# A hybrid decoder layer on one Trainium2 core: the first half's first two output-projection blocks made together, and a reordered piece of the first stage

## The chip, the cores and the metric

The kernel runs on one core of a Trainium2 chip. The metric is the device time of one execution in microseconds; the kernel before has a median of 2079.53 us over 3 runs (2077.59 to 2079.88). The profiled execution took 2081.88 us, of which 2080.0 us lie between its first and its last instruction. The engines are named as in the profile: PE (TensorE) multiplies matrices, PEld is its weight load, DVE is VectorE, ACT is ScalarE, POOL is GpSimd, SP issues the transfers, DMA carries them out.

## The reference, cut to what matters

One layer, 1024 tokens, width 1024, float32. Three branches share one input projection, are merged by sigmoid gates, and go through one output projection; a convolutional feed-forward block follows.

```
h = rms_norm(x, norm_mix_pre)
z = h @ w_in
y_pool = pool_branch(z_pool) @ w_proj_pool
y_mem  = mem_attention(z_q, mem_n) @ w_proj_mem
dw, da, dg = low-rank parts of the token-shifted z     # 64, 64 and 128 columns
w_log = -softplus(-(w0 + tanh(dw) @ w_up_decay)) - 0.5  # decay
a     = sigmoid(a0 + da @ w_up_a)
g     = sigmoid(dg) @ w_up_g                            # gate
y_rwkv = rwkv_branch(r, k, v, decay, a, g) @ w_proj_rwkv
gates  = sigmoid(z_gate + gate_b)
merged = gates[0] * y_pool + gates[1] * y_rwkv + gates[2] * y_mem
x = x + rms_norm(merged @ w_o, norm_mix_post)
u = causal_dwconv(rms_norm(x, norm_ffn_pre) @ w_ffn_up)
x = x + rms_norm((gelu(u_gate) * u_val) @ w_ffn_down, norm_ffn_post)
```

Two lines matter here: `tanh(dw)` and `sigmoid(dg)`, which are made in the first stage, and `merged @ w_o`.

## The kernel before, in words

Everything is held transposed: channels on the 128 partitions, tokens along the row. The 1024 channels are 8 rows of 128 (k = 0 to 7), the tokens two halves of 512 (n = 0, 1). A product of float32 quality is made of three PE passes with operands that are split into a high part and a rest: `mm3` (L165 to L171) does high by high (L168), rest of the activation by high weight (L169) and high activation by rest of the weight (L170). One output block (128 channels by 512 tokens) with all 8 rows is thus 24 matmuls into one PSUM bank; `gemm` (L173) runs over the rows.

Weights: `load_w` brings a block of 8 rows in four transfers of two rows each, issued by SP into `wraw` (3 buffers), then splits each: ACT makes the high part `whi` (L129), POOL the rest `wlo` (L132), 4 buffers each. There are two classes of all these buffers and of the PSUM banks (`g0`, `g1`, two banks each); successive blocks take the classes in turn. So the weights of one block can be prepared while another block is multiplied.

The stages around the change:

- First stage, `start()` (L367): the low-rank columns go into `lu` (decay part in partitions 0 to 63, the other in 64 to 127) and `gr` (gate). ACT makes tanh on the decay part; high parts and rests of it go into `la` and `ld` (L391, L392), the operands of two small products that come later, in `rwkv_group` (L454, L455). ACT also makes the sigmoid of `gr`, and its two parts go into `gl`, the operand of the gate's product `gl` by `w_up_g` right after it.
- `merge(n, js)` (L938): for output block j of half n, the product `y_rwkv` by `w_proj_rwkv` (8 rows, 24 matmuls), times the sigmoid of a gate `g` (L948), plus the other two branches' part (L949), then split by ACT into `mgh` (L122) and by DVE into `mgl` (L123). Block j of the merge is row k = j of the next product.
- `wo_gemm(n, js)` (L1106): the output projection, 8 blocks, each over the 8 rows `mgh`, `mgl`. Each finished block is copied to `o` by DVE (L1117), and its square is made by ACT (L1088 for block 0, L1091 for the others) and summed by DVE (L1092).
- After that the second half's merge begins, and the first half's residual and norm run beside it.

The program calls `merge(0, range(8))`, `wo_gemm(0, range(8))`, `merge(1, range(1))` and so on in this order. Within it, a scheduler sets the order of instructions on each engine from the code's order and from its own estimate of when operands are ready; each engine then works strictly through its row. The helper `two_gemms` (L289) makes two blocks together: rows 0 to `late`-1 of the first, the same rows of the second, then the remaining rows of the first and of the second. It is used in `merge(0, ...)`, for the first two blocks, with `late` = 6, and in `wo_gemm(1, ...)`, for the first two blocks, with `late` = 7.

## Time and profile before

| what | value |
|---|---|
| median of 3 runs | 2079.53 us (2077.59 to 2079.88) |
| the profiled execution | 2081.88 us, span 2080.0 us |
| PE busy | 2014.5 us, 97% of the span, 12246 matmuls |
| PEld | 1558.7 us, 75% |
| DVE, ACT, POOL busy | 1361.4 us (65%), 1069.4 us (51%), 812.5 us (39%) |
| mean granted TensorE clock | 0.992 of full speed |
| first half's output projection | first matmul at 1232.88 us, the next stage's first at 1281.30 us |
| last merge block's split of the first half | ACT at 1239.62 us, DVE at 1240.27 us |

In a timeline row, the first number is the start in us from the span's start, the second the duration; then the engine, the line, what is written and read, and in brackets the idle time before it and what ended it. Consecutive matmuls overlap in these rows: each is shown 0.39 us long, while the next starts 0.23 us after it. The distance between two starts is the time that one costs. In a list of waits the three numbers are the sum in us, the count and the longest.

### The profile page before, as it was taken

How to read it: one execution, taken by the hardware profiler on the slowest of the kernel's cores; microseconds unless marked ns; L12 is line 12 of the kernel's file. 1: busy time of each engine (PE TensorE's matmuls, PEld its weight loads, DVE VectorE, ACT ScalarE, POOL GpSimd, SP SyncE). 2: the span in 40 equal slices, each digit the busy share in tenths (PEclk: the TensorE clock that was granted, in tenths of full speed). 3: DMA queues.
4: the chain of work that ended last, by engine and by line, in shares of the span. 5: the costliest groups of instructions: out<-in, count | busy, mean ns of one | idle time of the engine just before them, and what ended most of it. 6: DMA issues, size and time to landing. Idle time of an engine off the chain costs nothing.

```text
span 2080.0 us, 34125 instructions
## 1 busy us (share of the span) xinstructions
PE 2014.5 (97%) x12246; PEld 1558.7 (75%) x12246; DVE 1361.4 (65%) x2170; ACT 1069.4 (51%) x2249; POOL 812.5 (39%) x917
## 2 busy tenths in 40 slices
PE   8999999999999999999999999998999999989997
PEld 5777767776778667866878878876678777767886
DVE  6567437664667357823895443778777777767798
ACT  7585348623773367434566243546444443444644
POOL 5521213121222121212133355655588888832341
PEclk9999999999999999999999999999999999999999
DMA  4312211120212021214427343634322222169776
GB/s 155 130 41 74 67 59 61 65 82 22 87 61 98 24 89 61 78 51 133 160 82 234 123 142 110 213 123 135 109 72 76 79 74 83 64 189 261 166 181 149
DMA packets 176713, 221.83 MB, mean 107 GB/s; under 512 B 16544, under 2 KB 128288, under 8 KB 176544
## 3 DMA queue, kind: packets, MB, share of 16 engines
q1 hardware_dynamic: 163616, 204.44, 30.3%
q0 software_dynamic: 11856, 14.16, 4.2%
q8 instruction: 97, 1.59, 0.3%
q10 hardware_dynamic: 1072, 1.05, 0.2%
q14 instruction: 72, 0.59, 0.1%
HBM read 170.30 MB, written 49.28 MB: 106 GB/s over the span
## 4 chain that ended last, share of the span: by engine, by line
PE 30%; DVE 7%; DMA 5%; POOL 4%; issue 4%; ACT 3%; SPq 0%; POOLq 0%; ACTq 0%; DVEq 0%
PE psg L170 5%; PE psg L169 5%; PE psg L168 5%; POOL wt L1028 2%; PE psd L169 2%; PE psd L170 2%; PE psf L170 2%; PE psd L168 2%; PE psf L169 2%; PE psf L168 2%; POOL sm L1013 1%; DMA a<-in_w_fup 1%; DMA g<-d_zg 1%; DMA R<-d_f 1%; POOL wlo L132 1%
## 5 line engine op out<-in xcount | busy, mean ns | idle before, releaser
L132 POOL TENSOR_TENSOR wlo<-wraw,whi 128x256 fp32r<-128x256 f32 x472 | 411.6, 881 | 941.8 <-ACT whi L129 775.1
L168 PE MATMUL psg<-hh,whi 128*128 128x512 f32 x928 | 380.7, 410 | 2.7 <-DVE kv L315 2.7
L170 PE MATMUL psg<-hh,wlo 128*128 128x512 f32 x928 | 376.9, 406 | 0.2
L169 PE MATMUL psg<-hl,whi 128*128 128x512 f32 x928 | 375.8, 405 | 0.0
L129 ACT CAST whi<-wraw 128x256 fp32r<-128x256 f32 x472 | 182.7, 403 | 220.8 <-PE psg L169 108.0
L168 PEld LDWEIGHTS psg<-hh,whi 128*128 128x128 f32 x928 | 174.7, 188 | 43.3 <-DVE kv L315 4.0
L170 PEld LDWEIGHTS psg<-hh,wlo 128*128 128x128 f32 x928 | 174.5, 188 | 43.2 <-POOL wlo L132 5.3
L169 PEld LDWEIGHTS psg<-hl,whi 128*128 128x128 f32 x928 | 174.7, 188 | 39.5 <-issue 3.4
L1028 POOL TENSOR_TENSOR wt<-a,wt 128x256 fp32r<-128x256 f32 x136 | 133.8, 1013 | 31.3 <-ACT wt L1027 31.3
L168 PE MATMUL psd<-f,u 128*128 128x512 f32 x292 | 115.8, 397 | 8.2 <-ACT f L1355 4.8
L169 PE MATMUL psd<-f,u 128*128 128x512 f32 x292 | 115.6, 396 | 0.6 <-DVE f L1359 0.6
L170 PE MATMUL psd<-f,u 128*128 128x512 f32 x292 | 115.2, 396 | 0.0
L1028 POOL TENSOR_TENSOR wt<-sm,wt 128x256 fp32r<-128x256 f32 x102 | 106.8, 1066 | 19.2 <-ACT wt L1027 19.2
L170 PE MATMUL psf<-h2h,wt 128*128 128x512 f32 x272 | 108.8, 400 | 1.0 <-POOL wt L1028 0.6
L168 PE MATMUL psf<-h2h,wt 128*128 128x512 f32 x272 | 106.3, 391 | 1.7 <-ACT wt L1027 1.6
L169 PE MATMUL psf<-h2l,wt 128*128 128x512 f32 x272 | 106.0, 390 | 0.0
L1027 ACT CAST wt<-sm 128x256 fp32r<-128x256 f32 x102 | 37.9, 404 | 129.4 <-POOL sm L1013 124.1
L1046 DVE SCALAR_TENSOR_TENSOR d<-z,pv,d 128x1023 f32<-128x1023 f32 x68 | 91.6, 1347 | 12.0 <-ACT d L1044 9.5
L170 PE MATMUL psf<-t,wt 128*128 128x512 f32 x204 | 80.8, 396 | 3.4 <-POOL wt L1028 3.4
L686 DVE TENSOR_TENSOR HV<-ph,Hd 64x128 f32<-64x128 f32 x112 | 32.4, 289 | 72.2 <-PE ph L640 48.0
L168 PE MATMUL psf<-t,wt 128*128 128x512 f32 x204 | 79.6, 390 | 0.0
L169 PE MATMUL psf<-t,wt 128*128 128x512 f32 x204 | 79.5, 390 | 0.0
(424 smaller groups left out, 4750.7 us busy)
## 6 DMA issues: line engine op xcount, KB each, us to landing
wraw<-in_w_in SPq DMA_DIRECT2D x240, 128.0 KB, 2.4
a<-in_w_fup SPq DMA_DIRECT2D x128, 128.0 KB, 2.4
d_zg<-st SPq DMA_DIRECT2D x48, 256.0 KB, 2.7
wraw<-in_w_fup SPq DMA_DIRECT2D x80, 128.0 KB, 2.5
fw<-in_w_fdn SPq DMA_DIRECT2D x33, 256.0 KB, 4.2
fraw<-d_f SPq DMA_DIRECT2D x33, 256.0 KB, 5.3
wraw<-in_w_prwkv SPq DMA_DIRECT2D x64, 128.0 KB, 2.4
wraw<-in_w_o SPq DMA_DIRECT2D x64, 128.0 KB, 2.5
```

The costliest lines, as they stand in the source:

```text
L129: last_whi[0] = A.copy(hi, src).ins
L132: (V if lo_on_dve[0] else G).tensor_tensor(lo, src, hi.bitcast(F32), op=ALU.subtract)
L168: first = PE.matmul(ps, wh, xh, start=start, stop=False)
L169: PE.matmul(ps, wh, xl, start=False, stop=False)
L170: last_mm[0] = PE.matmul(ps, wl, xh, start=False, stop=stop).ins
L686: ready = V.tensor_tensor(HV[q, :, c + 1, e], ph[q], Hd[q], op=ALU.add).ins
L1013: eng.tensor_tensor(out_[u], a[u], b[u], op=op)
L1027: A.copy(w[0][:, us], src[u])
L1028: last_low[0] = G.tensor_tensor(w[1][:, us], src[u], w[0][:, us].bitcast(F32), op=ALU.subtract).ins
L1046: V.scalar_tensor_tensor(d[:, n:], z[:, :T - n], col(cw, j), d[:, n:], op0=ALU.mult, op1=ALU.add)
```

## The change

Two edits. In `wo_gemm` the condition `n == 1 and j == 0` becomes `j == 0`: the first half's first two blocks are now made by `two_gemms` as well, with rows 0 to 6 of both ahead of row 7 of both. In `start()`, the five lines that make the tanh and the operands `la` and `ld` stand behind the gate's product instead of ahead of the gate's sigmoid.

```diff
@@ start() @@
             scaled(ev, 512, gemm(load_w(w_in[16 + 8 * c], KC, c=c), hrhs(512)))
-        act(u[0:64], u[0:64], AF.Tanh)
-        for q, o, l in ((slice(0, 64), slice(64, 128), ld), (slice(64, 128), slice(0, 64), la)):
-            A.copy(l[q], u[q])
-            V.tensor_tensor(l[o], u[q], l[q].bitcast(F32), op=ALU.subtract)
         act(gr[:, 0], gr[:, 0], AF.Sigmoid)
         split(gr[:, 0], gl[:, 0], gl[:, 1])
         split_w(gr[:, 1], gl[:, 2], gl[:, 3])
...
                 ev(t0, gemm(ws, lambda k: (gl[:, 0, t0:t0 + 512], gl[:, 1, t0:t0 + 512])))
+        act(u[0:64], u[0:64], AF.Tanh)
+        for q, o, l in ((slice(0, 64), slice(64, 128), ld), (slice(64, 128), slice(0, 64), la)):
+            A.copy(l[q], u[q])
+            V.tensor_tensor(l[o], u[q], l[q].bitcast(F32), op=ALU.subtract)
         normed(512, spills)
@@ wo_gemm() @@
             rhs = lambda k: (mgh[k][:, s], mgl[n][k])
-            if n == 1 and j == 0:
+            if j == 0:
                 two.extend(two_gemms([load_w(w_o[e], KC) for e in range(2)], rhs, KC - 1))
             ps = two.pop(0) if two else gemm(load_w(w_o[j], KC), rhs)
```

How the instructions move. On PE, in the first half's output projection, `mgh_12072` and `mgl_12529` are row 7 of the merged activations, `mgh_12071` and `mgl_12472` row 6. The piece below is the end of row 6 of the second block:

```order
 L169 MATMUL psg<-mgl_12472,whi 128x512
 L170 MATMUL psg<-mgh_12071,wlo 128x512
+L168 MATMUL psg<-mgh_12072,whi 128x512
+L169 MATMUL psg<-mgl_12529,whi 128x512
+L170 MATMUL psg<-mgh_12072,wlo 128x512
 L168 MATMUL psg<-mgh_12072,whi 128x512
 L169 MATMUL psg<-mgl_12529,whi 128x512
```

The three added rows are the first block's row 7. They stood 21 matmuls earlier, right behind row 6 of the first block and ahead of row 0 of the second. Nothing else moves on PE.

On ACT, at the same place of the program (`whi` are the high parts of weights, four casts to a block; `ss` and `sq` are the squares of finished output blocks; `mgh_12072` is row 7's high part):

```order
 L194 ACT_TABLE_LOAD
 L122 CAST mgh_12072<-g_12499 128x512
-L129 CAST whi<-wraw 128x256 x4
+L129 CAST whi<-wraw 128x256 x8
 L1088 ACTIVATE ss<-psg 128x512
-L129 CAST whi<-wraw 128x256 x4
 L1091 ACTIVATE sq<-psg 128x512
 L129 CAST whi<-wraw 128x256 x4
```

The square of block 0 now stands behind the casts of two blocks of weights (blocks 2 and 3) instead of one, directly ahead of the square of block 1.

On ACT in the first stage, where the five moved lines put their instructions:

```order
 L309 ACTIVATE lu<-psg,omu 128x512
 L200 ACTIVATE lu<-lu 64x1024
-L391 CAST la<-lu 64x1024
+L401 CAST la<-lu 64x1024
 L309 ACTIVATE gr<-psg,omu 128x512
-L391 CAST ld<-lu 64x1024
+L401 CAST ld<-lu 64x1024
 L200 ACT_TABLE_LOAD
 L200 ACTIVATE gr<-gr 128x1024
```

The tanh (`L200 ACTIVATE lu<-lu`) and both casts keep their places in the row; only the line number changes. The same holds for the two subtractions on DVE, and no other row of the first stage differs on any engine. POOL's and SP's rows are the same throughout.

## The prediction

> **What bounds the kernel now.** I read the page first, then the list of PE's own waits, then the timeline of the stage that is changed, engine by engine. The page says that PE is the engine to look at:

> ```profile
> PE 2014.5 (97%) x12246; PEld 1558.7 (75%) x12246; DVE 1361.4 (65%) x2170; ACT 1069.4 (51%) x2249; POOL 812.5 (39%) x917
> ```

> PE is busy 97% of the span. The change takes no matmul away, so all that it can win is a part of the 65.5 us in which PE stands still, and of what slow matmuls cost within the busy time. PE's waits over the whole span, the rows that bear on this case:

> ```profile
> PE psn L1097 <- DVE s L1092: 3.7, 1, 3.7
> ...
> PE psg L168 <- ACT mgh L122: 2.5, 1, 2.5
> PE psg L168 <- ACT whi L129: 2.3, 5, 1.3
> ...
> PE psg L169 <- DVE mgl L123: 0.2, 1, 0.2
> ```

> PE waits for a merged row exactly once for `mgh` and once for `mgl`. The timeline of PE shows where, and what else is lost there:

> ```profile
> 1232.88 0.39 PE L168 MATMUL psg<-mgh,whi 128*128 128x512 f32 x1
> ...
> 1237.41 0.39 PE L170 MATMUL psg<-mgh,wlo 128*128 128x512 f32 x1
> 1240.29 0.50 PE L168 MATMUL psg<-mgh,whi 128*128 128x512 f32 x1 [2.49 <-ACT mgh L122]
> 1241.02 0.50 PE L169 MATMUL psg<-mgl,whi 128*128 128x512 f32 x1 [0.22 <-DVE mgl L123]
> 1241.36 0.40 PE L170 MATMUL psg<-mgh,wlo 128*128 128x512 f32 x1
> 1241.60 0.58 PE L168 MATMUL psg<-mgh,whi 128*128 128x512 f32 x1
> 1241.97 0.63 PE L169 MATMUL psg<-mgl,whi 128*128 128x512 f32 x1
> 1242.40 0.63 PE L170 MATMUL psg<-mgh,wlo 128*128 128x512 f32 x1
> ...
> 1245.24 0.39 PE L168 MATMUL psg<-mgh,whi 128*128 128x512 f32 x1
> ...
> 1275.86 0.39 PE L168 MATMUL psg<-mgh,whi 128*128 128x512 f32 x1
> ...
> 1281.30 0.39 PE L168 MATMUL psg<-yh,whi 128*128 128x512 f32 x1
> ```

> The output projection of the first half begins at 1232.88 us and the next stage at 1281.30: 48.42 us for 192 matmuls. Its last block, 1275.86 to 1281.30, shows an undisturbed one: 5.44 us for 24, or 0.2267 us each. Eight such blocks are 43.52 us, so **4.90 us are lost here**, in three pieces. Row 7 would start at 1232.88 + 21 x 0.2267 = 1237.64 and starts at 1240.29: 2.65. From there to 1241.36 two matmuls take 1.07 instead of 0.45: 0.62, the wait for the rest. From 1241.36 to 1245.24 ten matmuls take 3.88 instead of 2.27: 1.61. In this third piece nothing is waited for; the matmuls themselves are slow, 0.43 us from 1241.97 to 1242.40, and the windows show a lower granted clock:

> ```profile
> 1238.00:1243.00 5.00, 2.49 (x7) 1.80 (x8) 1.38 (x2) 3.13 (x6) 2.31 (x3) 0.86 0.13 42
> 1243.00:1248.00 5.00, 5.00 (x20) 4.00 (x19) 0.00 (x0) 1.91 (x5) 2.37 (x4) 0.79 0.56 144
> 1248.00:1253.00 5.00, 5.00 (x24) 4.14 (x23) 1.53 (x2) 1.84 (x5) 3.08 (x4) 1.00 0.34 107
> ```

> The clock figure stands after the five engines' busy times: 0.86 and 0.79 behind the wait, 1.00 after it.

> **Part one, the two blocks together.** It removes and adds no instruction. Row 7 of block 0 goes behind 21 matmuls of block 1. When is row 7 ready, and is block 1 ready? The timelines of ACT, of DVE and of POOL in this stretch:

> ```profile
> 1236.41 0.41 ACT L129 CAST whi<-wraw 128x256 fp32r<-128x256 f32 x1 [2.07 <-DMA wraw<-in_w_o]
> 1237.68 0.63 ACT L200 ACTIVATE g<-g 128x512 f32<-128x512 f32 x1 [0.86 <-DMA g<-d_zg]
> 1238.32 1.28 ACT L194 ACT_TABLE_LOAD   x1
> 1239.62 0.62 ACT L122 CAST mgh<-g 128x512 fp32r<-128x512 f32 x1
> 1240.14 1.02 ACT L129 CAST whi<-wraw 128x256 fp32r<-128x256 f32 x3
> 1244.88 0.41 ACT L129 CAST whi<-wraw 128x256 fp32r<-128x256 f32 x1 [3.72 <-DMA wraw<-in_w_o]
> ...
> 1249.60 0.41 ACT L129 CAST whi<-wraw 128x256 fp32r<-128x256 f32 x1 [1.87 <-DMA wraw<-in_w_o]
> ...
> 1254.51 0.41 ACT L129 CAST whi<-wraw 128x256 fp32r<-128x256 f32 x1 [1.34 <-DMA wraw<-in_w_o]
> ```

> ```profile
> 1240.27 0.69 DVE L123 TENSOR_TENSOR mgl<-g,mgh 128x512 fp32r<-128x512 f32 x1 [3.87 <-ACT mgh L122]
> ```

> ```profile
> 1236.90 0.74 POOL L132 TENSOR_TENSOR wlo<-wraw,whi 128x256 fp32r<-128x256 f32 x1 [1.04 <-PE psg L169]
> ...
> 1245.36 2.22 POOL L132 TENSOR_TENSOR wlo<-wraw,whi 128x256 fp32r<-128x256 f32 x3 [2.43 <-ACT whi L129]
> ...
> 1250.08 2.58 POOL L132 TENSOR_TENSOR wlo<-wraw,whi 128x256 fp32r<-128x256 f32 x3 [1.54 <-ACT whi L129]
> ```

> The high part of row 7 is late because ACT first waits for a gate's transfer, makes its sigmoid and loads a table; all that stays in its row and none of it depends on the moved matmuls. So row 7 is ready at 1240.27 + 0.69 = 1240.96 in both kernels. PE will ask for it at 1232.88 + 42 x 0.2267 = 1242.40, 1.4 us later: all 2.65 + 0.62 us are covered, and with no idle PE the 1.61 us of slow clock have no cause. The cover is block 1, whose four weight pieces (the casts up to 1236.41) are complete when POOL ends at 1237.64; its first matmul needs only the first piece by then, and its last piece at 1237.64 + 18 x 0.2267 = 1241.72.

> Then everything arrives 4.9 us earlier at the supply of weights, and that is the next thing that could be late. PE reaches block 2 at 1232.88 + 48 x 0.2267 = 1243.76. Its last piece is cast by 1245.29, its rest made by 1245.36 + 0.74 = 1246.10; the first is needed at 1247.84, the second at 1248.29: 2.2 us to spare. The buffers of that piece are those of block 0's rows 6 and 7, now free at 1242.40 + 0.68 = 1243.08, still ahead of the cast. Block 3 is reached at 1249.20 and needs its last piece at 1253.28; before, it was cast at 1249.60 and its rest made from 1250.08 on. Block 4 is reached at 1254.64, last piece needed at 1258.72; before, cast at 1254.51. So even the old times of the supply would do, with 2 us or more in hand.

> The order of ACT also changes: the square of block 0 goes behind four more casts, to about 1250.0 instead of 1245.19. Until then block 0's PSUM bank is held, which block 4 takes (the class has two banks, and block 2 has the other); it is free about 1250.6 and needed at 1254.64, 4.0 us to spare. Behind the squares stand block 4's casts, which shift by less than 1 us. The price of this step is 0; if the 2.2 us of cover fails, the nearest row is PE's longest wait for a cast, 1.3 us.

> The sum for part one is -2.65 - 0.62 - 1.61 = -4.88; by the stage's total -4.90. From 1281.30 on, PE, the gates and the residual hang on this stage's end, so the gain is carried to the end if no later wait is tied to something else; bounds 3.3 (only the two waits) to 4.9.

> **Part two, the first stage.** The order of instructions shows no row moved on any engine, so its cost is 0 and its gain too. What it could touch is small anyway:

> ```profile
> 64.66 1.28 ACT L200 ACT_TABLE_LOAD   x1 [1.69 <-DVE gr L315]
> ...
> 61.98 1.32 DVE L392 TENSOR_TENSOR la<-lu,la 64x1024 fp32r<-64x1024 f32 x1
> 63.31 0.60 DVE L313 SCALAR_TENSOR_TENSOR gr<-zc,pv,gr 128x1 f32<-128x1 f32 x1
> ```

> The gate's table load at 64.66 waits for DVE's `gr`, ahead of which stands one subtraction for `la`; its 1.32 us are the most that moving it could give. I take 0.

> **Sum.** Span 2080.0 - 4.9 = 2075.1; the profiled execution's 2081.88 would be 2077.0. That execution lies 2.35 us above the median of the runs. Against the median: 2079.53 - 4.9 = **2074.6 us**.

> **Rivals.** (a) *The clock piece isn't won in a typical execution*, chance 0.24. Shorter idle times leave the clock alone, longer ones do not:

> ```profile
> 73.51 0.79 PE L168 MATMUL psg<-gl 128*128 128x512 f32 x1 [2.05 <-ACT st L325]
> 1409.45 2.08 PE L1097 MATMUL psn<-s,ones 128*128 128x512 f32 x2 [3.68 <-DVE s L1092]
> 1458.96 0.50 PE L170 MATMUL psg<-h2h,wlo 128*128 128x512 f32 x1 [1.62 <-POOL wlo L132]
> ```

> ```profile
> 60.00:80.00 20.00, 16.31 (x60) 12.03 (x58) 11.91 (x16) 12.57 (x20) 11.30 (x14) 0.83 0.32 107
> ...
> 1400.00:1420.00 20.00, 16.32 (x65) 12.33 (x64) 13.56 (x23) 9.61 (x19) 9.12 (x12) 0.91 0.60 190
> ...
> 1440.00:1460.00 20.00, 16.42 (x66) 11.60 (x65) 20.00 (x27) 11.89 (x26) 12.94 (x13) 1.00 0.26 83
> ```

> 1.62 us kept 1.00; 2.05 us (with smaller idle times around it) brought 0.83 and 3.68 us 0.91. So far the 2.49 us belong to those that pay. But this is one execution of each: where the same idle time doesn't pay in another, only the two waits are won, 2079.53 - 3.3 = 2076.2, less than 0.2%. The same size comes out if the later 3.68 us, reached 4.9 us earlier, cost one slow stretch of 1.6 us more than here. [...]

> (b) *The wait moves to the weights*: block 2's or 3's last piece is more than 2.2 us later than before because SP's or POOL's row is held by buffers that block 0 and 1 now free later. Against: those buffers are free before the old times of the casts. Price up to 1.3 us and no clock: 2075.9; chance 0.06.

> (c) *Slower*: ACT's square of block 0, now behind eight casts, releases the bank of block 4 late. It decides if the square ends after 1254.64, and the kernel is slower from 1259.5 on; a bank at 1264 would give 2079.53 + 4.5 = 2084.0. It needs block 3's last piece more than 9 us behind its old 1249.60, whereas the longest wait for a transfer in these rows is 3.72. Chance 0.03.

> (d) *Nothing is gained*: the 4.9 us come back at a later wait that does not move, 2079.5. The largest, for `s`, is DVE work begun behind this stage, so it moves too. Chance 0.05.

> **How the numbers follow.** The forecast has 0.62, the rivals 0.24, 0.06, 0.03, 0.05. About 0.2% (4.2 us) is what a measurement of this kernel can tell from no change. The forecast's 4.9 lies just beyond it; (a), (b) and (d) mostly within. A little of the forecast's mass falls inside by the runs' own spread of 2.3 us, a little of (b)'s outside: faster 0.60, same 0.36, slower 0.04. The range: below, the lowest run less the full gain, 2077.59 - 4.9 = 2072.7, taken as 2072.6; above, (a) plus the 2.0 us by which a single run lies off the median (2079.53 - 2077.59), 2078.2.

> **What would show it.** Right: in PE's waits the row for `mgh` is gone or below 0.3 us; the stage from the first `mgh` matmul to the next stage takes 43.5 us; the clock from 1238 to 1248 is 1.00; the table load in the first stage still waits for `gr` at 64.7. Wrong: a wait for `whi` or `wlo` within blocks 2 to 4; matmuls 0.43 us apart in the stage without an idle time before them; or a stage of 43.5 us and a later gap at 1400 or 1840 us longer than before.

## The result and the profile after

The changed kernel takes 2073.69 us (median of 9 runs, 2072.46 to 2075.89), against 2079.53 us (9 runs, 2077.59 to 2082.50) for the kernel before, measured beside it. The ratio is 0.9968, with a 95% interval of 0.9958 to 0.9978: 4.6 to 8.7 us faster. The forecast was 2074.6 us.

The profiled execution's span is 2071.9 us. In the list of PE's own waits (sum in us, count, longest), the rows for `mgh` and `mgl` are gone; the others that were shown of before stand:

```profile
PE psn L1097 <- DVE s L1092: 3.1, 1, 3.1
...
PE psg L168 <- ACT whi L129: 2.2, 4, 1.3
```

PE's timeline of the stage has no bracket with an idle time any more. First matmul of the output projection, and first of the next stage:

```profile
1231.23 0.39 PE L168 MATMUL psg<-mgh,whi 128*128 128x512 f32 x1
...
1274.75 0.39 PE L168 MATMUL psg<-yh,whi 128*128 128x512 f32 x1
```

That is 43.52 us for the 192 matmuls, to the hundredth what eight undisturbed blocks were worked out to take; before, it was 48.42. ACT's timeline shows that row 7 is no earlier than it was. Sigmoid, table load and the cast of row 7 stand there as before, and behind them the casts of two blocks and both squares in a row:

```profile
1236.53 0.63 ACT L200 ACTIVATE g<-g 128x512 f32<-128x512 f32 x1 [1.08 <-DMA g<-d_zg]
1237.18 1.28 ACT L194 ACT_TABLE_LOAD   x1
1238.48 0.62 ACT L122 CAST mgh<-g 128x512 fp32r<-128x512 f32 x1
1239.00 1.94 ACT L129 CAST whi<-wraw 128x256 fp32r<-128x256 f32 x6
1242.85 0.41 ACT L129 CAST whi<-wraw 128x256 fp32r<-128x256 f32 x1 [1.91 <-DMA wraw<-in_w_o]
1245.49 0.41 ACT L129 CAST whi<-wraw 128x256 fp32r<-128x256 f32 x1 [2.23 <-DMA wraw<-in_w_o]
1245.80 0.59 ACT L1088 ACTIVATE ss<-psg 128x512 f32<-128x512 f32 x1
1246.29 0.59 ACT L1091 ACTIVATE sq<-psg 128x512 f32<-128x512 f32 x1
```

The rest of row 7, on DVE:

```profile
1239.13 0.69 DVE L123 TENSOR_TENSOR mgl<-g,mgh 128x512 fp32r<-128x512 f32 x1 [4.12 <-ACT mgh L122]
```

Row 7 is ready at 1239.82 us; PE asks for it 42 matmuls after the stage's start, at 1231.23 + 42 x 0.2267 = 1240.75. The cover was 0.9 us (1.4 was forecast). Row 7's cast even came 7.25 us after the start of the stage, against 6.74 before; only the 21 matmuls in front of it hide that. The windows, with the granted clock after the five busy times:

```profile
1238.00:1243.00 5.00, 5.00 (x23) 4.13 (x22) 2.07 (x3) 3.08 (x9) 3.52 (x5) 1.00 0.19 59
1243.00:1248.00 5.00, 5.00 (x23) 4.13 (x22) 0.95 (x2) 2.55 (x7) 3.10 (x5) 1.00 0.58 189
```

PE is busy throughout and the clock is 1.00, where it had been 0.86 and 0.79. In the first stage, the gate's table load still waits for `gr`, and the casts stand where they stood:

```profile
62.18 1.04 ACT L401 CAST ld<-lu 64x1024 fp32r<-64x1024 f32 x1
64.89 1.28 ACT L200 ACT_TABLE_LOAD   x1 [1.68 <-DVE gr L315]
```

The two spans differ by 8.1 us, and the stage explains 4.90 of them. The rest lies in stages whose instructions are the same in both. One difference ahead of the change: PE's stage before the projection took 44.75 us in the one trace and 43.52 in the other, by a wait for `yl`. Behind it: from the next stage to the last matmul 787.93 us in the one and 786.30 in the other. The experiments show whether these belong to the change.

### The profile page after: what moved, and what is told of

It reads as the page before. It is cut to its first block, busy times and chain, and to the rows that moved or that the text cites. A ratio compares the mean times of both kernels' runs of the same rounds, so it can differ in the third digit from the quotient of the medians.

```text
span 2071.9 us, 34125 instructions
## 1 busy us (share of the span) xinstructions
PE 2011.4 (97%) x12246; PEld 1557.3 (75%) x12246; DVE 1362.5 (66%) x2170; ACT 1067.2 (52%) x2249; POOL 814.0 (39%) x917
## 4 chain that ended last, share of the span: by engine, by line
PE 31%; DVE 8%; POOL 4%; DMA 4%; issue 3%; ACT 2%; SPq 0%; POOLq 0%; DVEq 0%; ACTq 0%
PE psg L168 5%; PE psg L170 5%; PE psg L169 5%; POOL wt L1028 2%; PE psf L170 2%; PE psd L169 2%; PE psf L168 2%; PE psf L169 2%; PE psd L170 2%; PE psd L168 2%; POOL sm L1013 1%; DMA a<-in_w_fup 1%; DMA R<-d_f 1%; POOL wlo L132 1%; ACT d L1044 1%
## 5 line engine op out<-in xcount | busy, mean ns | idle before, releaser
L132 POOL TENSOR_TENSOR wlo<-wraw,whi 128x256 fp32r<-128x256 f32 x472 | 412.6, 885 | 936.0 <-ACT whi L129 756.7
L168 PE MATMUL psg<-hh,whi 128*128 128x512 f32 x928 | 380.7, 410 | 2.7 <-DVE kv L315 2.7
L170 PE MATMUL psg<-hh,wlo 128*128 128x512 f32 x928 | 376.7, 406 | 0.2
L169 PE MATMUL psg<-hl,whi 128*128 128x512 f32 x928 | 376.0, 405 | 0.0
L129 ACT CAST whi<-wraw 128x256 fp32r<-128x256 f32 x472 | 181.9, 403 | 225.7 <-PE psg L169 97.6
L168 PEld LDWEIGHTS psg<-hh,whi 128*128 128x128 f32 x928 | 174.8, 188 | 43.5 <-DVE kv L315 4.0
L170 PEld LDWEIGHTS psg<-hh,wlo 128*128 128x128 f32 x928 | 174.5, 188 | 42.6 <-POOL wlo L132 5.2
L169 PEld LDWEIGHTS psg<-hl,whi 128*128 128x128 f32 x928 | 174.7, 188 | 39.4 <-issue 3.6
L168 PE MATMUL psd<-f,u 128*128 128x512 f32 x292 | 115.9, 397 | 6.8 <-ACT f L1355 4.0
L169 PE MATMUL psd<-f,u 128*128 128x512 f32 x292 | 115.5, 396 | 0.4 <-DVE f L1359 0.4
L170 PE MATMUL psd<-f,u 128*128 128x512 f32 x292 | 115.1, 395 | 0.0
L170 PE MATMUL psf<-h2h,wt 128*128 128x512 f32 x272 | 108.8, 400 | 1.0 <-POOL wt L1028 0.6
L168 PE MATMUL psf<-h2h,wt 128*128 128x512 f32 x272 | 106.3, 391 | 0.1
L169 PE MATMUL psf<-h2l,wt 128*128 128x512 f32 x272 | 105.9, 389 | 0.0
L170 PE MATMUL psf<-t,wt 128*128 128x512 f32 x204 | 80.8, 396 | 3.2 <-POOL wt L1028 3.2
L168 PE MATMUL psf<-t,wt 128*128 128x512 f32 x204 | 79.5, 390 | 0.0
L169 PE MATMUL psf<-t,wt 128*128 128x512 f32 x204 | 79.5, 390 | 0.0
```

The lines of the kernel that those rows point to most:

```text
L129: last_whi[0] = A.copy(hi, src).ins
L132: (V if lo_on_dve[0] else G).tensor_tensor(lo, src, hi.bitcast(F32), op=ALU.subtract)
L168: first = PE.matmul(ps, wh, xh, start=start, stop=False)
L169: PE.matmul(ps, wh, xl, start=False, stop=False)
L170: last_mm[0] = PE.matmul(ps, wl, xh, start=False, stop=stop).ins
```

## The experiments

Every stage time below is from the start of the first `mgh` matmul to the start of the next stage's first matmul, in that kernel's own trace. The runs were made on other occasions than the first comparison, each group on a different chip; the kernel before, measured beside them, had medians of 2074.2 us (x1 to x4), 2071.9 us (x5 to x8) and 2076.4 us (x9, x10), so only ratios within a group are compared.

**x1: the second edit alone.**

```diff
-            if n == 1 and j == 0:
+            if j == 0:
```

> The second edit alone: wo_gemm makes the first half's blocks 0 and 1 together, start() is as before. Theory 1 (all of the gain is the covered wait in the first half's output projection): the stage from the first mgh matmul to the next stage takes 43.5 us instead of 48.4, and the time is that of the full change, ratio to before 0.997 (0.996 to 0.998). Theory 2 (the moved lines in the first stage bring the part of the measured 5.8 us that goes beyond 4.9): ratio 0.9977 or above, 4.9 us or less.

Stage 43.52 us. Ratio 0.9978 (0.9969 to 0.9987), 2069.58 us beside 2074.2. The time agrees with the full change within the intervals. It lies on the edge between the two theories' bounds and so does not separate them by itself.

**x2: the first edit alone.** The five lines of `start()` are moved, `wo_gemm` is as before.

> The first edit alone: the five lines in start() stand behind the gate's product, wo_gemm is as before. Theory 1 (no instruction changes its place on any engine, so nothing can change): ratio 1.000 within its interval, and the first stage as before, gate's table load waiting for gr at about 64.7 us. Theory 2 (the first stage gains the 0.9 us by which the medians differ from 4.9, or more): ratio 0.9996 or below, and the gate's product starting earlier than 68.1 us.

Ratio 0.9993 (0.9984 to 1.0002): no change that can be told. The point lies on the second theory's side (0.9996 or below), but the interval holds both theories, so the whole time does not separate them either. The first stage's table load waits as before:

```profile
63.88 1.28 ACT L200 ACT_TABLE_LOAD   x1 [1.68 <-DVE gr L315]
```

The gate's product began at 67.36 us here, earlier than the 68.1 that the second theory asked for. But it also began at 67.34 in x3, where the first stage is untouched, and at 68.84 in x5, so this is the spread between executions. What speaks for the first theory is the unchanged order of instructions, and that x1, without the moved lines, gains as much (0.9978) as x9 below with them (0.9982). What was not expected came in the output projection, whose instructions are here the same as in the kernel before: the stage took 45.89 us, not 48.4.

**x3 and x4: a smaller cover.** Row 7 of block 0 behind two rows of block 1 (x3) or one (x4), instead of seven:

```diff
...
-        for ks in (range(late), range(late, KC)):
-            for ws, ps in zip(wss, pss_):
-                for k in ks:
-                    mm3(ps, ws[k], rhs(k), k == 0, k == KC - 1)
+        for i, k0, k1 in ((0, 0, late), (1, 0, cover or late), (0, late, KC), (1, cover or late, KC)):
+            ws, ps = wss[i], pss_[i]
+            for k in range(k0, k1):
+                mm3(ps, ws[k], rhs(k), k == 0, k == KC - 1)
...
```

> As before, but row 7 of block 0 stands behind rows 0 and 1 of block 1 (6 matmuls, 1.36 us) and not behind all 7 rows. Row 7 is ready at the same time, so PE idles 2.65 - 1.36 = 1.3 us and then 0.6 for the rest. Theory 1 (the slow stretch comes from the long idle time): no slow stretch, clock 1.00, stage 43.5 + 1.9 = 45.4 us, time 3.0 us below before. Rival (the slow stretch has another cause, and would also have come without the wait): stage 47.0 us with matmuls 0.43 us apart, time 1.4 us below before.

> As before, but row 7 of block 0 stands behind row 0 of block 1 (3 matmuls, 0.68 us). PE idles 2.65 - 0.68 = 1.97 us, then 0.6. In the trace before, an idle time of 1.62 us kept the clock and one of 2.05 us (with others around it) lost it. If the clock is kept: stage 46.1 us, time 2.3 us below before. If it is lost: stage 47.7 us with about 8 matmuls 0.43 us apart, time 0.7 us below before. If only the wait counted and the clock were independent of it, 47.7 us too, in every one of these kernels, x3 included.

x3's wait in PE's timeline, then x4's:

```profile
1236.57 0.51 PE L168 MATMUL psg<-mgh,whi 128*128 128x512 f32 x1 [0.19 <-ACT mgh L122]
```

```profile
1239.80 0.51 PE L168 MATMUL psg<-mgh,whi 128*128 128x512 f32 x1 [1.55 <-ACT mgh L122]
```

x3: stage 44.51 us, clock 1.00, ratio 0.9995 (0.9983 to 1.0006). The idle time was 0.19 us and not 1.3, because row 7 came earlier in this execution: its cast began 5.79 us after the stage's start, against 6.74 in the trace of before. So this trace does not test what 1.3 us of idle time do to the clock. x4: stage 47.48 us, nearly the 47.7 of the case "clock lost", with eight matmuls 0.42 to 0.43 us apart; ratio 0.9997 (0.9988 to 1.0006). In x4 the clock fell (0.91 from 1230 to 1250 us) after 1.55 us of idle time, less than the 1.62 us that had kept it at 1.00 in the trace of before (1440 to 1460 us). The whole times tell neither kernel from before; 1.4 or 3.0 us cannot be settled with this spread.

**x5: the table load behind row 7's cast.** A manual order of two ACT instructions (`row7` is the cast of row 7's high part, which the merge hands on):

```diff
...
-    table(LN_EXP)
+    table(LN_EXP); later(phase[0], row7, True)
     res = wo_residual(0, pin)
```

> As before, but on ACT the table load L194 stands behind the cast of row 7's high part instead of ahead of it (a manual order of two ACT instructions; PE's order is as before). Row 7 is then ready 1.28 us earlier, or a little less, since one cast of weights comes ahead of it. Theory 1: PE idles 1.4 to 1.7 us plus 0.6 for the rest, clock 1.00, stage 45.5 to 45.8 us, time 2.6 to 2.9 us below before. If the clock is lost all the same: 47.1 to 47.4 us. If row 7 was late for another reason than ACT's row: stage 48.4 us.

ACT's timeline in x5:

```profile
1237.07 0.63 ACT L200 ACTIVATE g<-g 128x512 f32<-128x512 f32 x1 [0.76 <-DMA g<-d_zg]
1237.60 0.39 ACT L129 CAST whi<-wraw 128x256 fp32r<-128x256 f32 x1
1237.90 0.61 ACT L122 CAST mgh<-g 128x512 fp32r<-128x512 f32 x1
1238.53 1.28 ACT L194 ACT_TABLE_LOAD   x1
```

The cast stands 0.83 us behind the sigmoid's start, against 1.94 before: 1.1 us nearer. PE idled 1.57 us, as expected; the clock fell all the same (0.66 from 1238 to 1243 us), and the stage took 47.56 us (expected with it 47.1 to 47.4). Ratio 0.999 (0.9979 to 1.0001).

**x6: the wait filled.** Eleven extra matmuls between row 6 and row 7 of block 0, which goes through `two_gemms` alone here; nothing is done to make row 7 earlier. Of the edit, the line that matters:

```diff
...
         for ks in (range(late), range(late, KC)):
+            [PE.matmul(fill, wss[0][0][0], rhs(0)[0], start=True, stop=True) for _ in range(11 if fill is not None and ks[0] else 0)]
...
```

> As before, but PE does 11 extra matmuls (2.5 us, into a PSUM bank that is free, their product is not used) between row 6 and row 7 of block 0. Row 7 is ready as late as before, so nothing of the wait is won; PE only doesn't idle. Theory 1 (idle time lowers the clock, and that costs 1.6 us on top of the wait): clock 1.00, stage 43.5 + 2.65 + 0.62 = 46.8 us, time 1.6 us below before although PE has more to do. Rival (clock independent of the idle time): stage 48.4 us, time as before.

PE's timeline, and the windows row of the whole stretch:

```profile
1234.52 2.66 PE L293 MATMUL fill<-mgh,whi 128*128 128x512 f32 x11
```

```profile
1230.00:1250.00 20.00, 20.00 (x89) 16.43 (x88) 6.15 (x8) 8.27 (x20) 11.10 (x15) 1.00 0.39 123
```

Stage 46.08 us, clock 1.00 (46.8 was expected; row 7's cast began 6.02 us after the stage's start, not 6.74). No matmul of the stage is 0.43 us apart. In the whole time, 1.0005 (0.9995 to 1.0015), the 1.6 us that theory 1 expected are not seen: the interval reaches 1.0 us below before. One trace with the clock at 1.00 does not yet show that the fill kept it there, for x2 and x10 below have 1.00 without a fill.

**x7 and x10: the kernel before, twice more,** without an edit; x10 timed against itself.

> The kernel before, once more, for a second trace of it. If the slow stretch behind the wait belongs to the idle time of 2.5 us as such: stage 48.4 us again, clock 0.86 and 0.79 behind the wait. If it falls differently from run to run, stage 46.8 us in some traces. The other stretches with a lower clock (at 1405, 1840 and 1866 us) show by how much two traces of one kernel differ: expected 1.7 us steps.

> The kernel before timed against itself, to see what these comparisons tell from no change: ratio 1.000, and an interval of about 0.0010 to either side. Its trace is a fourth one of the same wait: stage between 45.9 and 48.4 us, with a slow stretch or without.

x10: 1.0006 (0.9995 to 1.0018). The wait for row 7 in PE's timeline of x7, then of x10, then of x2, whose program is the same here:

```profile
1239.12 0.49 PE L168 MATMUL psg<-mgh,whi 128*128 128x512 f32 x1 [1.97 <-ACT mgh L122]
```

```profile
1238.09 0.51 PE L168 MATMUL psg<-mgh,whi 128*128 128x512 f32 x1 [1.94 <-ACT mgh L122]
```

```profile
1236.46 0.49 PE L168 MATMUL psg<-mgh,whi 128*128 128x512 f32 x1 [1.57 <-ACT mgh L122]
```

The windows row from 1230 to 1250 us of x7 (the granted clock is the third number from the end), then of x10, then of x2:

```profile
1230.00:1250.00 20.00, 17.80 (x70) 13.98 (x69) 5.72 (x8) 9.47 (x21) 10.51 (x14) 0.91 0.39 126
```

```profile
1230.00:1250.00 20.00, 17.84 (x78) 14.22 (x77) 5.52 (x7) 9.54 (x22) 10.91 (x15) 1.00 0.36 111
```

```profile
1230.00:1250.00 20.00, 18.20 (x79) 14.54 (x78) 6.22 (x8) 8.17 (x20) 11.28 (x15) 1.00 0.36 116
```

1.97 us of idle time and a clock of 0.91, 1.94 us and 1.00: the same wait in the same program, once with the slow stretch and once without. Four traces of this stage, and what they lose against 43.52 us:

| trace | idle for `mgh` | slow stretch | stage | loss |
|---|---|---|---|---|
| before | 2.49 | yes | 48.42 | 4.90 |
| x7 | 1.97 | yes | 47.92 | 4.40 |
| x10 | 1.94 | no | 46.26 | 2.74 |
| x2 | 1.57 | no | 45.89 | 2.37 |

The mean loss is 3.6 us.

```profile
1237.22:1240.63 3.41, 1.27 (x4) 0.86 (x5) 0.70 (x2) 2.76 (x5) 1.17 (x2) 1.00 0.11 38
1240.63:1244.05 3.42, 3.42 (x9) 2.64 (x8) 0.68 (x1) 0.40 (x2) 1.13 (x2) 0.50 0.44 142
```

```profile
1234.34:1237.75 3.41, 1.81 (x8) 1.16 (x7) 0.00 (x0) 2.55 (x4) 0.74 (x1) 1.00 0.39 126
1237.75:1241.17 3.42, 2.86 (x11) 2.16 (x12) 1.39 (x2) 1.20 (x4) 2.32 (x3) 1.00 0.14 44
```

In x7 nearly all of the wait (1237.15 to 1239.12) lies within one window; PE is busy for 1.27 of its 3.41 us, and the next window has half the clock. In x10 the end of a window, at 1237.75, cuts the wait (1236.15 to 1238.09) in two, PE is busy for 1.81 and 2.86 us, and the clock stays at 1.00. In before, x4 and x5 the window with the wait has 1.13, 1.76 and 1.58 us of PE, and half the clock follows; in x2 the wait is cut as well, 2.13 and 2.90 us, and nothing follows. In the traces of before and after together, 1143 windows from 10 to 1990 us stand at the full clock. In seven of them PE is busy for 0.29 to 1.47 us, and each is followed by one at half the clock. Three have 1.75 (after), 1.78 and 1.79 us (before): the first two are followed by one, the third is not. In the other 1133 PE is busy for 1.93 us or more, and none is followed by one. Over all twelve traces, of 40 windows at the full clock with less than 1.64 us, 39 are followed by one at half the clock; of 6806 with more than 1.84 us none is, of the 25 between 10 are. These are counts of this program's traces; what in the chip makes it so they do not show. The busy times are approximate, since the ends of matmuls are modelled.

The idle time differs because the gate's sigmoid waits for its transfer: it starts 4.80 us after the stage's start in the trace of before (1237.68 - 1232.88), 4.28 in x7, 3.88 in x2 and 4.24 in x10, where ACT's timeline has

```profile
1235.47 0.63 ACT L200 ACTIVATE g<-g 128x512 f32<-128x512 f32 x1 [0.83 <-DMA g<-d_zg]
```

and the stage starts at 1231.23.

**x9: the full change again.**

> The full change once more, timed against the kernel before. So far the stage of the first half's output projection took 43.5 us in both traces with the second edit, and 48.4, 47.9 and 45.9 us in three traces of programs that are the same there as the kernel before: on the mean 3.9 us more. Theory 1 (that stage is all): ratio 0.998, that is 3.9 us, within 0.997 to 0.999. Theory 2 (something beyond that stage is won as well): ratio 0.997 or below.

Stage 43.52 us, as in the trace after and in x1 (and in x8 below). Ratio 0.9982 (0.9971 to 0.9994), 2072.44 us beside 2076.42, which is theory 1's number.

**x8: an attempt at the next wait.** The full change, and one feed-forward block ahead of the norm that waits for `s`:

```diff
-    steps = wo_norm(1, s2, last_mm[0])
+    d = up_block(3, 0, ahead.pop(0)); steps = wo_norm(1, s2, last_mm[0])
...
-        d = up_block(j, 0, ahead.pop(0))
+        d = up_block(j, 0, ahead.pop(0)) if n else d
```

> The full change, and in the second half one feed-forward block (block 3's gate part, 24 matmuls, 5.4 us) is put ahead of the norm's matmul psn that waits 3.1 to 3.7 us for the sum s of DVE, the largest wait left in the middle of the program. Hope: that wait and the slow clock behind it are covered, 3 to 5 us below the full change, about 2069. Against it: the norm starts up to 2 us later and with it the second half's activations h2h, for which fewer blocks are left as cover; the wait would then come back as one for h2h, and the time be that of the full change, 2073 to 2075, or some us above.

PE's timeline, the norm's matmul and the waits behind it:

```profile
1403.98 1.02 PE L1097 MATMUL psn<-s,ones 128*128 128x512 f32 x2
...
1418.37 0.57 PE L168 MATMUL psg<-h2h,whi 128*128 128x512 f32 x1 [2.44 <-ACT whi L129]
1430.94 0.49 PE L168 MATMUL psg<-h2h,whi 128*128 128x512 f32 x1 [0.92 <-ACT h2h L122]
...
1433.45 0.49 PE L168 MATMUL psg<-h2h,whi 128*128 128x512 f32 x1 [1.06 <-ACT h2h L122]
1435.14 0.50 PE L169 MATMUL psg<-h2l,whi 128*128 128x512 f32 x1 [1.20 <-DVE h2l L123]
```

The norm no longer waits, and 2.44 + 0.92 + 1.06 + 1.20 = 5.6 us of waits for weights and for `h2h`, `h2l` take its place. From 1395 to 1500 us PE stands still for 9.9 us in x8, against 10.3 in the trace after and 9.4 in x9: the wait moved. The ratio to before is 0.998 (0.9971 to 0.9989), as for the full change in x9; no full change was timed in this group, so a small difference between the two cannot be told.

## Why the prediction was right, and where it was not

**The wait and its cover.** Right. PE waited for row 7 in every trace of the old order, and in this stage of none of the four traces of the new one (after, x1, x8, x9); the stage takes 43.52 us each time.

**The weights, the squares and the bank** (rivals b and c). Right that they cost nothing: PE has no wait in the stage. Block 0's square ended at 1245.80 + 0.59 = 1246.39 in the trace after, not at 1250.6: ACT's casts were quicker through than estimated: six of the eight ran in one go from 1239.00 us, and only two waited for transfers (1242.85 and 1245.49). Block 4 began at 1231.23 + 96 x 0.2267 = 1252.99.

**The slow clock.** Right, as far as the traces go, that it goes with idle time: in those of before and after, each of the nine stretches at half the clock up to 1990 us begins behind a window in which PE was busy for at most 1.78 of 3.41 us, and with PE busy throughout this stage (after, x1, x8, x9, x6) the clock there is 1.00. x6 by itself doesn't show it: without the fill PE would have idled for 1.8 us by estimate (x2's 1.57, and a cast 0.2 us later), and the end of a window at 1235.9 us would have cut that, as in x2. That it costs 1.61 us in a typical execution, which the sum took, does not hold: two of four traces of the same stage paid it. The step that failed is the reading "Shorter idle times leave the clock alone, longer ones do not", by which the 2.49 us "belong to those that pay". 1.55 and 1.57 us lost the clock in x4 and x5; 1.57 and 1.94 us kept it in x2 and x10. What the traces show in its place is a difference in where the wait falls: nearly whole within one window it left PE busy there for 1.13 us (before), 1.27 (x7), 1.76 (x4) and 1.58 (x5), and half the clock followed; cut in two, with 1.81 and 2.86 us (x10) or 2.13 and 2.90 us (x2), it was followed by none. This is rival (a), to which 0.24 was given: it is no alternative to the forecast but a part of each set of runs. The steps of 3.413 us lie elsewhere in each trace: counted from the span's start, the first slow stretch begins at 70.87 us in before, at 70.62 in after and at 69.86 in x7.

**The size of the sum.** -4.90 was one execution's loss, at the upper end of four (2.37 to 4.90, mean 3.6). The wait itself was mis-sized as a constant too: 1.57 to 2.49 us of idle time, by when the gate's transfer lands. The first comparison gave more than the sum (0.9968, 6.7 us), the repeats 4.6 us (x1) and 3.7 us (x9). The first interval, from 4.6 us, does not hold the mean of 3.6 by itself; the intervals of x1 (2.7 to 6.4) and x9 (1.2 to 6.0) do. So the forecast of 2074.6 came close to 2073.69 partly because an effect taken too large met a comparison that came out large. Whether something beyond the stage is won in the first comparison stays open; no trace shows a place for it. The stage ahead of the projection, whose instructions are the same in all, took 44.75, 43.90, 44.06 and 43.52 us in before, x7, x10 and x2, and 43.52, 43.52 and 43.60 in after, x1 and x9; but it took 43.52 to 43.54 us in x3 to x6 too, so its wait for `yl` comes and goes without the change.

**The first stage.** Right: 0. The order of instructions is unchanged, and x1 without the moved lines gains as much as x9 with them. x2's interval alone would still hold 3.3 us of gain.

**Nothing comes back later** (rival d). From the next stage to the last matmul, the traces with the old order took 787.9, 782.9, 785.2 and 783.2 us (before, x7, x10, x2), those with the new one 786.3, 785.9 and 783.2 (after, x1, x9). Both spread over some 3 to 5 us, and the gain isn't given back there as a rule. The 1.6 us by which the first two traces differ behind the stage are within this spread.

## What to carry to other kernels

Where the last operand of a product is late, the matmuls of the next output block over the operands already there are a full cover (here with 0.9 us to spare), as long as its weights and its bank are ready; the order on the other engines shows what then comes later, and it must have room. Before an edit is costed, look at the order that the scheduler makes of it: one of these two edits moved no instruction at all. And a wait read from one trace is one draw: here the same wait cost between 2.4 and 4.9 us, so its price is better read from several traces.

## What was not expected of the hardware

Almost the same idle time of PE, in the same place of the same program, is followed by a half-speed stretch in one execution and not in another (1.97 us with it in x7, 1.94 us without in x10). The two traces differ in how the idle time falls on steps of 3.413 us, on which the slow stretches of a trace begin: in x7 nearly all of it lies between two steps, with 1.27 us of PE work in 3.41 us, and the next 3.41 us had half the clock; in x10 a step cuts it in two, with 1.81 and 2.86 us of PE work, and the clock stayed at 1.00. In this stage 1.55 us of idle time, with the 0.22 us for the rest behind them, were followed by a slow stretch where nearly all fell between two steps (x4), and 1.94 us were not where they were cut in two (x10). Why it is so was not shown. The stretch costs about 1.6 us: in x7, from 1240.66 on, eight matmuls 0.42 to 0.43 us apart instead of 0.23. It is most of what the traces of this stage differ by.
